# Differential attention: the query by key-low-part products as 64-row matmuls, both components scored in one step

## The chip, the cores and the metric

One core of one Trainium2 chip. The metric is the device time of one execution in microseconds (us), the median of several runs. TensorE (PE) multiplies, VectorE (DVE), ScalarE (ACT) and GpSimd (POOL) work on tiles of 128 partitions, and SyncE (SP) issues the transfers.

## What is computed

A block of two mixers over 2048 tokens of width 1024, followed by a sliding-window layer. The change lies in the first block's differential attention, with four heads of two components of 64 each:

```python
def diff_attention(q, k, v, lam, slopes):
    """q, k: (B,S,H,2,Dh) normalised; v: (B,S,H,2Dh). Returns (B,S,H,2Dh)."""
    ...
    def block(args):
        qblk, qp = args
        s = jnp.einsum('bqhce,bkhce->bchqk', qblk, k).astype(jnp.float32) * scale
        dist = jnp.abs(qp[:, None] - pos[None, :]).astype(jnp.float32)
        s = s - slopes[:, None, None] * dist
        a = jax.nn.softmax(s, axis=-1)
        w = a[:, 0] - lam * a[:, 1]
        return jnp.einsum('bhqk,bkhe->bqhe', w.astype(v.dtype), v)
```

So for each head and each block of 128 queries there are two score matrices of 128 x 2048, two softmaxes, their difference, and one product with v.

## The kernel before, in words

Every fp32 operand of a product is split into a high part and a low part, both in TensorE's rounded fp32, and a product is the sum of partial products in PSUM. Phase a projects x to q, k, v and z and writes the parts to DRAM. Phase b1 (`phase_b1`) is the differential attention, phase b2 (`phase_b2`) the dilated attention; then follow the output projection and the second layer.

Phase b1 goes through 64 steps g: 4 heads of 16 query tiles. The two components of a head are numbered e. A query tile `qst` holds component e's high part in partitions 0 to 63 and its low part in 64 to 127, for 512 queries. A key tile `kst` holds one part (i = 0 high, 1 low) of one component of 512 keys, twice: in partitions 0 to 63 and again in 64 to 127. One 128-row matmul therefore gives (q high + q low) times one key part, and two of them, accumulated, a score block of 128 x 512.

`scores(g, e, hf)` fills one PSUM tile `s_ps` of 128 x 1024, half hf of component e's row, with four matmuls (L322), and VectorE reads it once (L328): it adds the position bias, writes `et` in SBUF and keeps the running row maximum `mx`. There are four such fills in a step and 256 in the phase. The pool `b_ps` has two such tiles, so TensorE can fill one while VectorE reads the other. After both halves of a component, `exps` (L336, L338) applies the exponential on ScalarE; after both components, `combine` (L344 to L356) subtracts the weighted second from the first on GpSimd (in the last TAIL = 2 steps on VectorE).

Three steps later (LT = 3) `transposes` turns the result by 128 x 128 pieces on TensorE (L366), ScalarE writes the high part `pth` (L367) and VectorE the low part `ptl` (L368). Two steps after that `pv` (L380 to L382) multiplies with v, 24 matmuls of 256 columns a step. `evacuate` and `finish` (L386 to L414) normalise four tiles at a time: ScalarE, a chain of short VectorE instructions (`rsqrt_dve`, L238 to L256), GpSimd, and the store `s_y<-b_an`.

A list scheduler orders each engine's instructions when the program is built; the source's order is its priority. Loads go through SP's queue: `load_k` (L296) for a head, `load_q` (L309) for 512 queries, `load_v`.

Pools of a phase lie behind each other in SBUF in the order of its `with`. Phase b2's pools take the same addresses over, and one of them can be written only when the pools of b1 that lie there are free. The first three of b1, `b_c`, `b_q0` and `b_k0` (the bias, two query tiles, 20 key tiles), take 8.25 + 4 + 40 = 52.25 KB of a partition; behind them come `b_t2` (two `et` tiles of component 1), and later `b_v`, `b_p` (`pth`, `ptl`) and `b_o` (`b_ot`, `b_an`). Phase b2's first pool `d_h0` (queries, keys and values of a head) takes 41.5 KB and its second, `d_b` (the bias tables `d_nb`, `d_rb`, `d_two`), the next 9.25 KB; `d_p` (`d_nh`, `d_nl`, `d_ph`, `d_pl`) lies over `b_v` and `b_p`. Phase b2's `load` (L516 to L525) fetches a head, `scores_nat` (L541, L544) and `scores_res` (L564, L567) score it.

Of the kernel before, what the change touches and what calls it, by code (L numbers as in the profile page):

```python
# [16 lines left out]
P = 128  # L17
S = 2048
D = 1024
NT = S // P  # L20
# [2 lines left out]


def rsqrt_mean(nc, c, pool, ss, n, out=None):
    """1 / sqrt(ss / n + eps), refined by one Newton step."""
    w = ss.shape[-1]
    sd = pool.tile([P, w], F32, name="rm_sd")
    nc.scalar.activation(sd, ss, AF.Sqrt, bias=c["eps"], scale=1.0 / n)
    v = pool.tile([P, w], F32, name="rm_v")  # L30
    nc.vector.tensor_scalar(v, ss, 1.0 / n, EPS, ALU.mult, ALU.add)
    nc.vector.reciprocal(sd, sd)
    nc.vector.tensor_mul(v, v, sd)
    nc.vector.tensor_mul(v, v, sd)
# [196 lines left out]


def rsqrt_dve(nc, pool, ss, n, out=None):
    """1 / sqrt(ss / n + eps) on VectorE alone: exponent-halving start, three Newton steps (the
    first leaves -2 y, the second 16 y, and the third takes the factor out)."""
    w = ss.shape[-1]
    v = pool.tile([P, w], F32, name="rd_v")
    nc.vector.tensor_scalar(v, ss, 1.0 / n, EPS, ALU.mult, ALU.add)  # L238
    sh = pool.tile([P, w], I32, name="rd_i")
    nc.vector.tensor_scalar(sh, v.bitcast(I32), 1, None, ALU.logical_shift_right)  # L240
    y = pool.tile([P, w], F32, name="rd_y")
    nc.vector.tensor_scalar(y.bitcast(I32), sh, -1.0, float(0x5F3759DF), ALU.mult, ALU.add)
    a = pool.tile([P, w], F32, name="rd_a")
    if out is None:
        out = y
    for step in range(3):
        if w == 1:
            nc.vector.tensor_scalar(a, v, y, y, ALU.mult, ALU.mult)
        else:
            nc.vector.tensor_mul(a, y, y)  # L250
            nc.vector.tensor_mul(a, a, v)
        if step < 2:
            nc.vector.scalar_tensor_tensor(y, a, (3.0, 12.0)[step], y, ALU.subtract, ALU.mult)
        else:
            nc.vector.tensor_scalar(a, a, -0.5 / 4096, 1.5 / 16, ALU.mult, ALU.add)
            nc.vector.tensor_mul(out, y, a)  # L256
    return out


def phase_b1(tc, c, scr, ndist, sub_g, lam):  # L260
    nc = tc.nc
    NQ = 4 * NT
    with (
        tc.tile_pool(name="b_c", bufs=1) as cp,
        tc.tile_pool(name="b_q0", bufs=2) as qp0,
        tc.tile_pool(name="b_k0", bufs=20) as kp0,
        tc.tile_pool(name="b_t2", bufs=2) as tp2,
        tc.tile_pool(name="b_s", bufs=8) as sp,
        tc.tile_pool(name="b_t0", bufs=3) as tp0,
# [13 lines left out]
        bias = cp.tile([P, 3968], mybir.dt.float16, name="nd")  # L283
# [4 lines left out]

        heads, qts, st, pts, outs = {"n": 0}, {}, {}, {}, {}

        def load_k(h, e, j):
            for i in range(2):
                t = (kp0 if heads["n"] % 22 < 20 else kp1).tile([P, 512], F32R, name="kst")
                heads["n"] += 1
                for half in range(2):
                    nc.sync.dma_start(t[64 * half:64 * half + 64].bitcast(F32),  # L296
                                      scr["dk"][h, e, i][:, j * 512:j * 512 + 512])
                heads[h, "k", e, i, j] = t

        def load_v(h, j):  # L300
            t = vp.tile([P, 4, 2, 128], F32R, name="vt")
# [2 lines left out]
            heads[h, "v", j] = t  # L304

        def load_q(h, b):
            for e in range(2):
                t = (qp0, qp1)[b % 2].tile([P, 512], F32R, name="qst")
                nc.sync.dma_start(t.bitcast(F32),  # L309
                                  scr["dq"][h, e].rearrange("s d t -> (s d) t")[:, b * 512:b * 512 + 512])  # L310
                qts[h, b, e] = t

        def scores(g, e, hf):
            h, qt = divmod(g, NT)
            if e == 0 and hf == 0:
                st[g] = {"e": [pool.tile([P, 2, 1024], F32, name="et") for pool in (tp1 if g % 4 == 3 else tp0, tp3 if g % 3 == 2 else tp2)], "l": sp.tile([P, 2], F32, name="l")}
            et = st[g]["e"][e]
            lhs = qts[h, qt // 4, e][:, (qt % 4) * P:(qt % 4 + 1) * P]
            ps = ps_s.tile([P, 1024], F32, name="s_ps")
            for b in range(2):  # L320
                for i in range(2):
                    nc.tensor.matmul(ps[:, b * 512:b * 512 + 512], lhs, heads[h, "k", e, i, 2 * hf + b],  # L322
                                     start=i == 0, stop=i == 1)
            if hf == 0:
                st[g]["mx"] = sp.tile([P, 2], F32, name="mx")
            mx = st[g]["mx"]
            off = 1920 - qt * P + hf * 1024
            nc.vector.tensor_tensor_reduce(  # L328
                et[:, hf], ps, bias[:, off:off + 1024], 1.0,
                -3.0e38 if hf == 0 else mx[:, 0:1], ALU.add, ALU.max, mx[:, hf:hf + 1])  # L330

        def exps(g, e):
            slope = DIFF_SLOPES[g // NT]
            et, mx = st[g]["e"][e], st[g]["mx"]
            nm = sp.tile([P, 1], F32, name="nm")
            nc.scalar.activation(nm, mx[:, 1:2], AF.Copy, scale=-slope)  # L336
            ev = et.rearrange("p a k -> p (a k)")
            nc.scalar.activation(ev, ev, AF.Exp, bias=nm, scale=slope, accum_out=st[g]["l"][:, e:e + 1])  # L338
# [76 lines left out]
                    scr["y"][0][b * 512:(b + 1) * 512, h * 128:(h + 1) * 128].rearrange("(t p) w -> p t w", p=P), an)  # L415

        load_q(0, 0)
        for e in range(2):
            for j in range(4):
                load_k(0, e, j)  # L420
        for g in range(NQ + LT + 5):
            h, qt = divmod(g, NT)
            if g < NQ and qt == 0:
                for j in range(4):
                    load_v(h, j)
            if g < NQ and qt % 4 == 1:
                ng = g + 3
                if ng < NQ:
                    load_q(ng // NT, (ng % NT) // 4)
            for s in range(4):  # L430
                e, hf = divmod(s, 2)
                if g < NQ:
                    with tc.high_priority(offset=AHEAD) if g < EARLY else nullcontext():
                        scores(g, e, hf)
                    if qt == NT - 1 and h < 3 and hf == 1:
                        for j in range(4):
                            load_k(h + 1, e, j)
                if 0 <= g - LT < NQ:
                    transposes(g - LT, s)
                p, half = divmod(g - LT - 2, 2)  # L440
                if 0 <= p < NQ // 2:
                    for kt in range(8 * half + 2 * s, 8 * half + 2 * s + 2):
                        pv(p, kt)
                if s == FIN and half == 0 and 0 <= p - 1 < NQ // 2:
                    finish(p - 1)
                if g < NQ and hf == 1:
                    with tc.high_priority(offset=AHEAD) if g < EARLY else nullcontext():
                        exps(g, e)
            if g < NQ:
                with tc.high_priority(offset=AHEAD) if g < EARLY else nullcontext():  # L450
                    combine(g)
            p, half = divmod(g - LT - 2, 2)
            if half == 1 and 0 <= p < NQ // 2:
                evacuate(p)
# [312 lines left out]
def phase_c(tc, c, scr, x, p, w_out, ple_g, w_gate, w_proj, norm_g):  # L767
    nc = tc.nc
    with (
# [13 lines left out]
        wo, wg, wj = {}, {}, {}  # L783
# [6 lines left out]
            store[k, ch] = w  # L790

        def to_t(src_of, dst, cuts):
            """transpose 128-column pieces, cuts[i]:cuts[i + 1] at a time, and split them into dst[:, 0] and dst[:, 1]"""
            for b, m in zip(cuts, [e - b for b, e in zip(cuts, cuts[1:])]):
                ps = pt.tile([P, 4, P], F32, name="c_tp")
                for j in range(m):
                    nc.tensor.transpose(ps[:, j], src_of(b + j), c["id"])
                nc.scalar.activation(dst[:, 0, b:b + m], ps[:, :m], AF.Copy)
                nc.vector.tensor_sub(dst[:, 1, b:b + m], ps[:, :m], dst[:, 0, b:b + m].bitcast(F32))
# [529 lines left out]
```

## Time and profile before

| | us |
|---|---|
| median of 3 runs | 3122.9 (3122.07 to 3132.4) |
| profiled execution, span from first to last instruction | 3126.1 |
| PE busy (share of the span) | 2988.1 (96%) |
| weight loads busy | 2499.6 (80%) |
| DVE busy | 1980.9 (63%) |
| ACT busy | 1591.5 (51%) |
| POOL busy | 1165.9 (37%) |

The span is the profiled execution's own; nothing that lies around it is given apart. It is 3.2 us above the median of the runs and inside their spread. Busy time of PE is modelled with the matmuls' latency in it, so that a PE busy for 96% isn't at its peak. The shares are averages over stages: phase b1 lies from about 740 to 1450 us, phase b2 behind it to about 1850 us.

### The profile page before, as it was taken

What the parts mean: (1) busy time and instruction counts of PE and PEld (TensorE: products, weight loads), DVE (VectorE), ACT (ScalarE), POOL (GpSimd) and SP (SyncE); (2) the same over time, 40 slices, a digit from 0 to 9 for tenths busy, and PEclk for the clock granted to TensorE, in tenths of its full rate; (3) what the DMA queues carried; (4) which work ended last, traced back from release to release, by engine and by line L of the source; (5) the groups of instructions that cost most, each with busy time, mean ns of one, the idle gap of its engine ahead of it and who ended that gap; (6) DMA issues with size and microseconds to landing.
All of it is one profiled execution on the core that took longest, in us unless ns stands there. A gap on an engine that the chain in (4) does not pass through costs nothing.

```text
span 3126.1 us, 45716 instructions
## 1 busy us (share of the span) xinstructions
PE 2988.1 (96%) x15778; PEld 2499.6 (80%) x15778; DVE 1980.9 (63%) x4986; ACT 1591.5 (51%) x3528; POOL 1165.9 (37%) x1052
## 2 busy tenths in 40 slices
PE   8999999999988888988999989999999999999998
PEld 7788888887877777777887867888888888888787
DVE  4215555423999999997787765444445666666765
ACT  5223233312877666776877753222235666666621
POOL 1110011110876667763454540000035565555421
PEclk9999999999999999998999999999999999999999
DMA  7654444415131211106757563233273424232452
GB/s 211 126 132 102 104 118 118 111 61 174 30 91 39 81 55 48 54 15 154 173 143 163 123 167 112 88 107 105 89 238 97 155 88 155 88 116 80 130 190 84
DMA packets 421928, 352.78 MB, mean 113 GB/s; under 512 B 104480, under 2 KB 367168, under 8 KB 418624
## 3 DMA queue, kind: packets, MB, share of 16 engines
q1 hardware_dynamic: 421552, 348.83, 39.8%
q8 instruction: 126, 2.06, 0.3%
q0 software_dynamic: 144, 1.02, 0.2%
q14 instruction: 106, 0.87, 0.1%
HBM read 234.26 MB, written 116.52 MB: 112 GB/s over the span
## 4 chain that ended last, share of the span: by engine, by line
PE 80%; DVE 11%; DMA 4%; issue 2%; ACT 2%; SPq 1%; POOL 0%; DVEq 0%; ACTq 0%; POOLq 0%
PE psm L181 7%; PE psm L183 7%; PE psm L182 7%; PE e_mm L762 5%; PE e_mm L764 5%; PE s_ps L322 5%; PE e_mm L763 4%; PE c_mm L762 4%; PE c_mm L763 4%; PE c_mm L764 4%; DVE et L328 4%; PE d_sr L564 4%; PE t_ps L366 2%; PE f_mm L762 2%; PE f_mm L763 2%
## 5 line engine op out<-in xcount | busy, mean ns | idle before, releaser
L181 PE MATMUL psm<-w,hh 128*128 128x512 f32 x1024 | 406.3, 398 | 9.9 <-DVE t L111 7.1
L183 PE MATMUL psm<-w,hh 128*128 128x512 f32 x1024 | 399.5, 393 | 0.0
L182 PE MATMUL psm<-w,hl 128*128 128x512 f32 x1024 | 399.3, 391 | 0.0
L982 POOL TENSOR_TENSOR e_wt<-e_raw,e_wt 128x1024 fp32r<-128x1024 f32 x80 | 191.3, 2398 | 478.1 <-DMA e_raw<-in_a_w_in_dram 403.9
L322 PE MATMUL s_ps<-kst,qst 128*128 128x512 f32 x1024 | 309.3, 429 | 55.2 <-DVE mx L328 54.6
L101 POOL TENSOR_TENSOR w<-wraw,w 128x512 fp32r<-128x512 f32 x64 | 81.6, 1297 | 599.6 <-ACT w L100 589.6
L356 POOL TENSOR_TENSOR et<-et 128x1024 f32<-128x1024 f32 x124 | 295.1, 2401 | 0.0
L322 PEld LDWEIGHTS s_ps<-kst,qst 128*128 128x128 f32 x1024 | 187.3, 202 | 103.7 <-DVE mx L328 77.1
L338 ACT ACTIVATE et<-et,nm 128x2048 f32<-128x2048 f32 x128 | 257.0, 2007 | 5.7
L181 PEld LDWEIGHTS psm<-w,hh 128*128 128x128 f32 x1024 | 193.3, 189 | 48.5 <-DVE t L111 7.5
L762 PE MATMUL e_mm<-e_x,e_wt 128*128 128x512 f32 x576 | 228.1, 396 | 1.3 <-DVE e_k L1024 0.9
L764 PE MATMUL e_mm<-e_x,e_wt 128*128 128x512 f32 x576 | 226.8, 394 | 0.0
L763 PE MATMUL e_mm<-e_x,e_wt 128*128 128x512 f32 x576 | 226.6, 393 | 0.0
L183 PEld LDWEIGHTS psm<-w,hh 128*128 128x128 f32 x1024 | 192.9, 189 | 41.1
L182 PEld LDWEIGHTS psm<-w,hl 128*128 128x128 f32 x1024 | 193.7, 189 | 38.3
L355 POOL TENSOR_SCALAR et<-et,cc 128x1024 f32<-128x1024 f32 x124 | 138.4, 1131 | 215.8 <-DVE cc L346 122.9
L366 PE MATMUL t_ps<-id,et 128*128 128x128 f32 x1024 | 163.2, 289 | 21.0 <-DVE ptl L368 19.8
L1070 DVE CUSTOM_DVE_ANT_0 e_es<-e_s,e_bias,e_sk 128x256 f32<-128x256 f32 (+1 forms) x256 | 117.3, 472 | 104.1 <-PE e_s L1062 73.5
L1083 POOL TENSOR_SCALAR e_es<-e_es,e_l 128x256 f32<-128x256 f32 (+1 forms) x256 | 119.6, 488 | 170.2 <-DVE e_l L1081 105.2
L367 ACT ACTIVATE pth<-t_ps 128x512 fp32r<-128x512 f32 x256 | 146.4, 590 | 62.8 <-PE t_ps L366 57.7
L368 DVE TENSOR_TENSOR ptl<-t_ps,pth 128x512 fp32r<-128x512 f32 x256 | 170.5, 681 | 12.0 <-ACT pth L367 11.6
L328 DVE CUSTOM_DVE_ANT_0 et<-s_ps,nd,mx 128x1024 f32<-128x1024 f32 x128 | 163.5, 1277 | 19.9 <-PE s_ps L322 18.3
(265 smaller groups left out, 7936.6 us busy)
## 6 DMA issues: line engine op xcount, KB each, us to landing
e_raw<-in_a_w_in_dram SPq DMA_DIRECT2D x80, 512.0 KB, 3.6
wraw<-in_w_in_dram SPq DMA_DIRECT2D x64, 256.0 KB, 3.4
kst<-s_dk SPq DMA_DIRECT2D x128, 128.0 KB, 3.8
d_k<-s_bk SPq DMA_DIRECT2D x32, 512.0 KB, 12.0
s_xt<-c_at SPq DMA_DIRECT2D x32, 512.0 KB, 6.5
e_x<-s_xt SPq DMA_DIRECT2D x32, 512.0 KB, 6.9
t<-in_x_dram SPq DMA_DIRECT2D x32, 256.0 KB, 5.4
s_dv<-t SPq DMA_DIRECT2D x32, 256.0 KB, 3.1
```

The lines of the kernel that those rows point to most:

```text
L181: nc.tensor.matmul(ps, ah, cur[k][:, 0], start=k == 0, stop=False)
L182: nc.tensor.matmul(ps, al, cur[k][:, 0], start=False, stop=False)
L183: nc.tensor.matmul(ps, ah, cur[k][:, 1], start=False, stop=k == KD - 1)
L322: nc.tensor.matmul(ps[:, b * 512:b * 512 + 512], lhs, heads[h, "k", e, i, 2 * hf + b], start=i == 0, stop=i == 1)
L328: nc.vector.tensor_tensor_reduce(et[:, hf], ps, bias[:, off:off + 1024], 1.0, -3.0e38 if hf == 0 else mx[:, 0:1], ALU.add, ALU.max, mx[:, ...
L338: nc.scalar.activation(ev, ev, AF.Exp, bias=nm, scale=slope, accum_out=st[g]["l"][:, e:e + 1])
L356: nc.gpsimd.tensor_sub(es[0][:, hf], es[0][:, hf], es[1][:, hf])
L366: nc.tensor.transpose(pt[:, j], src[:, (4 * (kg % 2) + j) * P:(4 * (kg % 2) + j + 1) * P], c["id"])
L762: nc.tensor.matmul(ps, ah, bh, start=first, stop=False)
L763: nc.tensor.matmul(ps, al, bh, start=False, stop=False)
L764: nc.tensor.matmul(ps, ah, bl, start=False, stop=last)
L982: nc.gpsimd.tensor_sub(w[:, 1], raw, w[:, 0].bitcast(F32))
```

## The change

The low parts of the keys of both components go into one tile, component 0 in partitions 0 to 63 and component 1 in 64 to 127, and the low product uses the query's high part alone, with 64 rows: rows 0 to 63 for component 0, 64 to 127 for component 1. For this the query tile of component 1 is loaded with its parts exchanged. What is no longer computed is q low times k low. `scores` now fills two PSUM tiles, one of each component; a head has 12 key tiles for 16, and `b_k0` shrinks to 16 tiles.

```diff
-        tc.tile_pool(name="b_k0", bufs=20) as kp0,
+        tc.tile_pool(name="b_k0", bufs=16) as kp0,
...
-        def load_k(h, e, j):
-            for i in range(2):
-                t = (kp0 if heads["n"] % 22 < 20 else kp1).tile([P, 512], F32R, name="kst")
+        def load_k(h, j):
+
+            for nm, parts in (("k0", ((0, 0), (0, 0))), ("k1", ((1, 0), (1, 0))), ("kl", ((0, 1), (1, 1)))):
+                t = (kp0 if heads["n"] % 18 < 16 else kp1).tile([P, 512], F32R, name="kst")
                 heads["n"] += 1
-                for half in range(2):
+                for half, (e, i) in enumerate(parts):
                     nc.sync.dma_start(t[64 * half:64 * half + 64].bitcast(F32),
                                       scr["dk"][h, e, i][:, j * 512:j * 512 + 512])
-                heads[h, "k", e, i, j] = t
+                heads[h, nm, j] = t
...
             for e in range(2):
                 t = (qp0, qp1)[b % 2].tile([P, 512], F32R, name="qst")
-                nc.sync.dma_start(t.bitcast(F32),
-                                  scr["dq"][h, e].rearrange("s d t -> (s d) t")[:, b * 512:b * 512 + 512])
+                for i in range(2):
+                    half = i ^ e
+                    nc.sync.dma_start(t[64 * half:64 * half + 64].bitcast(F32),
+                                      scr["dq"][h, e, i][:, b * 512:b * 512 + 512])
                 qts[h, b, e] = t
...
-            ps = ps_s.tile([P, 1024], F32, name="s_ps")
+            lhs = [qts[h, qt // 4, e][:, (qt % 4) * P:(qt % 4 + 1) * P] for e in range(2)]
+            ps = [ps_s.tile([P, 1024], F32, name="s_ps") for _ in range(2)]
+            for e in range(2):
+                for b in range(2):
+                    nc.tensor.matmul(ps[e][:, b * 512:b * 512 + 512], lhs[e], heads[h, f"k{e}", 2 * hf + b],
+                                     start=True, stop=False)
             for b in range(2):
-                for i in range(2):
-                    nc.tensor.matmul(ps[:, b * 512:b * 512 + 512], lhs, heads[h, "k", e, i, 2 * hf + b],
-                                     start=i == 0, stop=i == 1)
...
+                for e in range(2):
+                    rows = slice(64 * e, 64 * e + 64)
+                    nc.tensor.matmul(ps[e][:, b * 512:b * 512 + 512], lhs[e][rows], heads[h, "kl", 2 * hf + b][rows],
+                                     start=False, stop=True)
             off = 1920 - qt * P + hf * 1024
-            nc.vector.tensor_tensor_reduce(
-                et[:, hf], ps, bias[:, off:off + 1024], 1.0,
-                -3.0e38 if hf == 0 else mx[:, 0:1], ALU.add, ALU.max, mx[:, hf:hf + 1])
+            for e in range(2):
+                mx = st[g]["mx"][e]
+                nc.vector.tensor_tensor_reduce(
+                    st[g]["e"][e][:, hf], ps[e], bias[:, off:off + 1024], 1.0,
+                    -3.0e38 if hf == 0 else mx[:, 0:1], ALU.add, ALU.max, mx[:, hf:hf + 1])
...
             for s in range(4):
-                e, hf = divmod(s, 2)
-                if g < NQ:
+                if g < NQ and s % 2 == 0:
                     with tc.high_priority(offset=AHEAD) if g < EARLY else nullcontext():
-                        scores(g, e, hf)
-                    if qt == NT - 1 and h < 3 and hf == 1:
-                        for j in range(4):
-                            load_k(h + 1, e, j)
+                        scores(g, s // 2)
+                    if qt == NT - 1 and h < 3:
+                        for j in range(s, s + 2):
+                            load_k(h + 1, j)
...
-                if g < NQ and hf == 1:
+                if g < NQ and s >= 2:
                     with tc.high_priority(offset=AHEAD) if g < EARLY else nullcontext():
-                        exps(g, e)
+                        exps(g, s - 2)
```

What the scheduler makes of it is read from the built programs. First, TensorE's queue in the middle of phase b1, before; `s_ps` is the PSUM tile that is filled, `kst` a key tile, `qst` a query tile, and the numbers tell tiles apart.

```order
L322 MATMUL s_ps_9810<-kst_8106,qst_9155 128x512
L322 MATMUL s_ps_9810<-kst_8109,qst_9155 128x512
L322 MATMUL s_ps_9810<-kst_8112,qst_9155 128x512
L322 MATMUL s_ps_9810<-kst_8115,qst_9155 128x512
L322 MATMUL s_ps_9845<-kst_8010,qst_9153 128x512
L322 MATMUL s_ps_9845<-kst_8013,qst_9153 128x512
L322 MATMUL s_ps_9845<-kst_8016,qst_9153 128x512
L322 MATMUL s_ps_9845<-kst_8019,qst_9153 128x512
L366 MATMUL t_ps_9854<-id_60,et_9508 128x128 x4
```

The same place now, two fills again; L327 are the 128-row products with the keys' high part, L332 the 64-row products.

```order
L375 MATMUL t_ps_8609<-id_60,et_8241 128x128 x4
L327 MATMUL s_ps_8597<-kst_7993,qst_8235 128x512
L327 MATMUL s_ps_8597<-kst_8002,qst_8235 128x512
L332 MATMUL s_ps_8597<-kst_7999,qst_8235 128x512
L332 MATMUL s_ps_8597<-kst_8008,qst_8235 128x512
L327 MATMUL s_ps_8598<-kst_7996,qst_8238 128x512
L327 MATMUL s_ps_8598<-kst_8005,qst_8238 128x512
L332 MATMUL s_ps_8598<-kst_7999,qst_8238 128x512
L332 MATMUL s_ps_8598<-kst_8008,qst_8238 128x512
L375 MATMUL t_ps_8622<-id_60,et_8241 128x128 x4
```

In the source the four 64-row products stand together, component 0 and 1 in turn. In the queue they stand tile by tile: two products of 128 rows, two of 64 rows in one half of the array, then the other component's. Over the whole phase the queue goes 514 times from 128 rows to 64 or back, and in 3 places a 64-row product of one component is next to one of the other.

Second, SP's queue where phase b1 ends, before (`d_q`, `d_k`, `d_vn`, `d_vr` are phase b2's first head, `d_nb` to `d_rb` its bias tables, `s_y` the stores of b1's output).

```order
L396 DMA b_sz<-s_sz 128x4x128
L487 DMA d_nb<-in_t_nat_dram 128x256
L489 DMA d_rb_14047<-in_t_res_dram 128x128
L491 DMA d_two<-in_t_two_dram 128x128
L495 DMA d_rb__14051<-in_t_res_dram 128x896
L495 DMA d_rb__14053<-in_t_res_dram 128x896
L516 DMA d_q<-s_bq 128x2048
L414 DMA s_y_137<-b_an 128x4x128
L519 DMA d_k_14057<-s_bk 64x2048 x2
```

And now:

```order
L526 DMA d_k_14042<-s_bk 64x2048 x2
L528 DMA d_vn_14045<-s_bv 128x15x128
L529 DMA d_vn_14045<-s_bv 64x128
L530 DMA d_vn_14045<-s_bv 64x128
L423 DMA s_y_137<-b_an 128x4x128
L532 DMA d_vr<-s_bv 128x16x128
L494 DMA d_nb<-in_t_nat_dram 128x256
L496 DMA d_rb_14031<-in_t_res_dram 128x128
```

The tables have moved behind the whole first head and behind a store, because `d_b` now lies over `b_t2`.

Third, ScalarE's queue at the first `d_ph` (phase b2's probabilities, pool `d_p`), with what the instructions wait for, before and now:

```order
L408 ACTIVATE b_j,b_ssq<-b_an 128x128 [waits Activation_49]
L599 ACTIVATE d_ph<-d_tr 128x4x128 [waits DMAHW1_49,PE_49]
L599 ACTIVATE d_ph<-d_tr 128x4x128 [waits PE_49]
L582 ACTIVATE d_pn<-d_tn 128x512 [waits PE_49,Pool_49]
L623 ACTIVATE d_o_14103<-d_ob 128x4x64 [waits PE_49]
```

```order
L422 ACTIVATE b_an<-b_an,rd_y 128x128 [waits DVE_49,Pool_49]
L422 ACTIVATE b_an<-b_an,rd_y 128x128 x2
L422 ACTIVATE b_an<-b_an,rd_y 128x128 [waits Activation_49]
L555 ACTIVATE d_en,d_o_14087<-d_en,d_nmn 128x256 [waits DVE_49,PE_49]
L555 ACTIVATE d_en,d_o_14087<-d_en,d_nmn 128x256
L606 ACTIVATE d_ph<-d_tr 128x4x128 [waits DMAHW3_49,DMAHW4_49,DMAHW1_49,DMAHW6_49,DMAHW0_49,Activation_49]
```

`d_p` now ends inside `b_o`, so that the first `d_ph` stands behind the last scaling of `b_an` (L422, L413 before) and waits for five queues of transfers, where it waited for one.

## Rows read from the trace of the kernel before

**Rows 1.** The page: each engine's busy time, share of the span, number of instructions.

```profile
PE 2988.1 (96%) x15778; PEld 2499.6 (80%) x15778; DVE 1980.9 (63%) x4986; ACT 1591.5 (51%) x3528; POOL 1165.9 (37%) x1052
```

**Rows 2.** Busy time by stretch: stretch and length, then busy us by engine, granted clock.

```profile
core 0: us, PE busy (x) PEld busy (x) DVE busy (x) ACT busy (x) POOL busy (x), PEclk, DMA share, GB/s
...
790.00:1420.00 630.00, 556.65 (x3416) 482.11 (x3417) 586.69 (x1019) 448.72 (x853) 455.71 (x270) 0.93 0.17 50
1420.00:1480.00 60.00, 49.46 (x296) 41.93 (x294) 42.30 (x146) 39.33 (x114) 13.90 (x14) 0.84 0.71 173
```

**Rows 3.** Groups by line, 790 to 1420 us: busy, mean ns; idle before, releaser.

```profile
L322 PE MATMUL s_ps<-kst,qst 128*128 128x512 f32 x959 | 289.4, 428 | 52.8 <-DVE mx L328 52.1
...
L328 DVE CUSTOM_DVE_ANT_0 et<-s_ps,nd,mx 128x1024 f32<-128x1024 f32 x120 | 153.3, 1277 | 19.2 <-PE s_ps L322 17.8
...
L328 DVE CUSTOM_DVE_ANT_0 et<-s_ps,nd 128x1024 f32<-128x1024 f32 x119 | 144.6, 1215 | 16.8 <-PE s_ps L322 13.6 <-POOL et L356 1.4 <-POOL et L355 0.6
```

**Rows 4.** Who waited for whom, 790 to 1420 us: total, times, longest.

```profile
PE s_ps L322 <- DVE mx L328: 52.1, 41, 5.0
...
DVE et L328 <- PE s_ps L322: 31.4, 50, 1.9
...
PE t_ps L366 <- DVE ptl L368: 17.1, 11, 2.7
...
DVE r L344 <- ACT et L338: 3.8, 10, 0.6
...
PE t_ps L405 <- DVE ptl L368: 3.7, 3, 1.2
```

**Rows 5.** The chain that ended last, 790 to 1420 us, shares by line.

```profile
by line: PE s_ps L322 21.8%; DVE et L328 18.0%; PE t_ps L366 9.7%; DVE ptl L368 7.4%; issue 7.2%; PE o_ps L380 5.4%; PE o_ps L381 5.3%; PE o_ps L382 5.3%; DVE rd_a L250 4.2%; DVE rd_a L251 3.4%; DVE rd_a L255 3.0%; DVE rd_y L242 2.5%; DVE r
```

**Rows 6.** Timeline of PE's matmuls in phase b2: start, us, line, rows*columns of the weights.

```profile
1823.06 0.28 PE L611 MATMUL d_or<-d_nl,d_vn 128*64 128x256 f32 x1
1823.17 0.28 PE L611 MATMUL d_or<-d_nh,d_vn 128*64 128x128 f32 x2
1823.29 0.22 PE L611 MATMUL d_or<-d_nl,d_vn 128*64 128x128 f32 x1
1823.45 0.46 PE L706 MATMUL d_ob<-id,d_ta 64*128 64x64 f32 x4
1823.83 2.10 PE L564 MATMUL d_sr<-d_k,d_q 128*128 128x512 f32 x4
```

**Rows 7.** The same view, another place in phase b2.

```profile
1504.81 0.22 PE L611 MATMUL d_or<-d_nl,d_vn 128*64 128x128 f32 x1
1504.87 1.16 PE L564 MATMUL d_sr<-d_k,d_q 128*128 128x512 f32 x2
1505.97 0.46 PE L706 MATMUL d_ob<-id,d_ta 64*128 64x64 f32 x4
1506.36 0.66 PE L579 MATMUL d_tn<-id,d_en 128*128 128x128 f32 x4
1506.85 0.60 PE L597 MATMUL d_tr<-id,d_er 128*128 128x128 f32 x4
```

**Rows 8.** Lines' instructions: ns min/median/max, first and last start; L322 in phase b1.

```profile
L322 PE MATMUL s_ps<-kst,qst x959: 387/393/797, 789.9 to 1419.6; 128*128 128x512 f32 x192
...
L706 PE MATMUL d_ob<-id,d_ta x128: 221/223/275, 1494.2 to 1842.3; 64*128 64x64 f32 x128
```

**Rows 9.** Timeline of all engines, a fill in phase b1.

```profile
1126.62 1.09 PE L322 MATMUL s_ps<-kst,qst 128*128 128x512 f32 x4
```

**Rows 10.** Timeline where phase b1 ends (brackets: idle before, releaser).

```profile
1423.74 1.27 DVE L328 CUSTOM_DVE_ANT_0 et<-s_ps,nd,mx 128x1024 f32<-128x1024 f32 x1
...
1440.76 0.55 PE L541 MATMUL d_sn<-d_k,d_q 128*128 128x256 f32 x1 [7.14 <-DMA d_k<-s_bk]
...
1446.98 0.42 DVE L544 CUSTOM_DVE_ANT_0 d_en<-d_sn,d_nb 128x256 f32<-128x256 f32 x1 [0.83 <-issue]
```

**Rows 11.** SP's queue in the same stretch: start, us in the queue.

```profile
1444.27 0.60 SPq L525 DMA_DIRECT2D d_vr<-s_bv  x1
1456.68 0.36 SPq L414 DMA_DIRECT2D s_y<-b_an  x1
...
1493.11 0.37 SPq L414 DMA_DIRECT2D s_y<-b_an  x1
```

**Rows 12.** The first d_ph on ACT: ns min/median/max, first and last start.

```profile
L599 ACT ACTIVATE d_ph<-d_tr x128: 574/597/607, 1468.0 to 1836.3; 128x512 fp32r<-128x512 f32 x128
```

**Rows 13.** Issues by line: count, KB each, median us to landing.

```profile
kst<-s_dk SPq DMA_DIRECT2D x128, 128.0 KB, 3.8
d_k<-s_bk SPq DMA_DIRECT2D x32, 512.0 KB, 12.0
...
s_y<-b_an SPq DMA_DIRECT2D x16, 256.0 KB, 2.3
```

More of the change, by code (lines that the diff above doesn't have):

```diff
@@ L308, in load_q, with scores @@
                 t = (qp0, qp1)[b % 2].tile([P, 512], F32R, name="qst")
-                nc.sync.dma_start(t.bitcast(F32),
-                                  scr["dq"][h, e].rearrange("s d t -> (s d) t")[:, b * 512:b * 512 + 512])
+                for i in range(2):
+                    half = i ^ e
+                    nc.sync.dma_start(t[64 * half:64 * half + 64].bitcast(F32),
+                                      scr["dq"][h, e, i][:, b * 512:b * 512 + 512])
                 qts[h, b, e] = t
-        def scores(g, e, hf):
+        def scores(g, hf):
@@ L314, in scores @@
             h, qt = divmod(g, NT)
[L315 to L318, printed above, removed]
-            ps = ps_s.tile([P, 1024], F32, name="s_ps")
-            for b in range(2):
-                for i in range(2):
-                    nc.tensor.matmul(ps[:, b * 512:b * 512 + 512], lhs, heads[h, "k", e, i, 2 * hf + b],
-                                     start=i == 0, stop=i == 1)
@@ L324, in scores @@
-            if hf == 0:
-                st[g]["mx"] = sp.tile([P, 2], F32, name="mx")
-            mx = st[g]["mx"]
-            off = 1920 - qt * P + hf * 1024
-            nc.vector.tensor_tensor_reduce(
-                et[:, hf], ps, bias[:, off:off + 1024], 1.0,
-                -3.0e38 if hf == 0 else mx[:, 0:1], ALU.add, ALU.max, mx[:, hf:hf + 1])
+            if hf == 0:
+                st[g] = {"e": [pool.tile([P, 2, 1024], F32, name="et") for pool in (tp1 if g % 4 == 3 else tp0, tp3 if g % 3 == 2 else tp2)],
+                         "l": sp.tile([P, 2], F32, name="l"),
+                         "mx": [sp.tile([P, 2], F32, name="mx") for _ in range(2)]}
@@ L332, in exps @@
+            off = 1920 - qt * P + hf * 1024
+            for e in range(2):
[3 more added lines that the diff above has]
+                    -3.0e38 if hf == 0 else mx[:, 0:1], ALU.add, ALU.max, mx[:, hf:hf + 1])
         def exps(g, e):
             slope = DIFF_SLOPES[g // NT]
-            et, mx = st[g]["e"][e], st[g]["mx"]
+            et, mx = st[g]["e"][e], st[g]["mx"][e]
@@ L417, in phase_b1 @@
         load_q(0, 0)
-        for e in range(2):
-            for j in range(4):
-                load_k(0, e, j)
+        for j in range(4):
+            load_k(0, j)
         for g in range(NQ + LT + 5):
@@ L430, in phase_b1 @@
             for s in range(4):
-                e, hf = divmod(s, 2)
-                if g < NQ:
+                if g < NQ and s % 2 == 0:
                     with tc.high_priority(offset=AHEAD) if g < EARLY else nullcontext():
-                        scores(g, e, hf)
-                    if qt == NT - 1 and h < 3 and hf == 1:
-                        for j in range(4):
-                            load_k(h + 1, e, j)
+                        scores(g, s // 2)
+                    if qt == NT - 1 and h < 3:
+                        for j in range(s, s + 2):
+                            load_k(h + 1, j)
                 if 0 <= g - LT < NQ:
```

## Prediction

> **What bounds the kernel now.** The page says that TensorE is busy for 96% of the span [rows 1], which is an average over stages, so the next view is the busy time of the stretch that the change lies in, 790 to 1420 us [rows 2]. There VectorE has 586.7 of 630 us and TensorE 556.7: neither is full, and the reader is to see two engines that hand the two PSUM tiles to and fro. The waits say how [rows 4]: TensorE waits 52.1 us for a reduction (`mx`) before a fill, in 41 waits, and 17.1 and 3.7 us for `ptl` before transposes, 72.9 us in all; VectorE waits 31.4 us for a fill. The chain through the stretch [rows 5] goes through both, 21.8% in the fills and 18.0% in the reductions. A microsecond taken from either is worth less than one here, and one added costs less than one.
>
> **What the change does to the matmuls.** The phase has 1024 score matmuls of 512 columns before and after; half of them now have 64 rows. A fill of four takes 1.09 us, its last one 0.39 [rows 8, 9], so one step is (1.09 - 0.39) / 3 = 0.23 us. The trace has no 64-row matmul of 512 columns. Steps in it go with the columns: 0.06 us for 128, 0.11 for 256 [rows 6]. So I take 0.23 for 64 rows too, and a gain of 0 from the rows alone. The other end is that the two halves of the array work side by side: then 256 pairs save 256 x 0.23 = 59 us of TensorE. That needs the two components' low products next to each other in the queue, and the built queue has them so in 3 places; everywhere else the scheduler has finished one PSUM tile before it begins the other, because the second tile comes free only when VectorE has read it.
>
> **What it adds: 514 changes between 128 and 64 rows.** Before, phase b1 has none. Phase b2 has some, in the 64-row transposes of `d_ob`. The last 128-column matmul ahead of one starts at 1823.29 and the transpose at 1823.45 [rows 6]: 0.16 us, where its neighbours of the same size take 0.06. That is 0.10 us of nothing. On the way back, the fourth transpose starts 0.46 - 0.22 = 0.24 us after the first [rows 6, 8], at 1823.69, and the next 128-row matmul at 1823.83, 0.14 later for 64 columns, which should take at most 0.06: 0.08 or more. Rows 7 repeat this (1506.21 to 1506.36). I take 0.09 a change. Behind a change the first weight load isn't hidden: four transposes take 0.66 us and the next four 0.60 [rows 7], which is 0.06 more. A change costs 0.09 + 0.06 = 0.15 us, and 514 of them 77.1 us of TensorE. A change of columns costs nothing (64 to 128 columns from 1504.81 to 1504.87, the plain step of 0.06 [rows 7]), so it is the rows.
>
> The Trainium skill, TensorEngine Tiling (Array Packing), Key Properties, says that changing the tiling mode, and not just the tile, drains TensorE. For rows the trace agrees, with the 0.09 us; for columns it doesn't, with the 0.06 us that is a plain step. By that rule the gap belongs to each of the 514 changes and not to a wait of the transposes, which is the more reason to take it for all.
>
> **How much of it lies on the path.** The chain has 21.8% of 630 us, 137.3 us, in the fills [rows 5], of 289.4 us that they are busy [rows 3]: 47%. In that share of the fills TensorE is the one that is late, and what is added there moves the end; in the rest it waits for VectorE anyway. 0.47 x 77.1 = 36 us. The ends are 77.1 - 72.9 = 4 us, if all of TensorE's idle time took up what is added, and 77 us, if nothing did. I take 36, by the row that is about these very instructions. The granted clock is 0.93 in the stretch [rows 2], so some of it runs at 1.2 GHz instead of 2.4 and a change may cost more there than in phase b2; the upper end has room for it.
>
> **The reductions and exponentials.** Their number and sizes stay (1277 and 1215 ns [rows 3]). Component 0's exponential now follows the third reduction of a step instead of the second, and component 1's comes right behind it. The result is read three steps later, and a step takes 630 / 60 = 10.5 us (239 reductions at 4 a step), so I cost this at 0; if that cover were too short, VectorE's wait for ScalarE (3.8 us [rows 4]) would double: +4.
>
> **The loads.** `kst` goes from 128 to 96 issues, `qst` from 32 of 256 KB to 64 of 128 KB. The transfer engines are at 0.17 in the stretch [rows 2] and no wait for a key tile stands in rows 4: cost 0, at worst one landing of 3.8 us [rows 13] at each of 3 changes of head, 11 us.
>
> **Where the phase ends.** Four key tiles fewer move all later pools by 8 KB. Two things follow in the built order. First, phase b2's tables are loaded behind its first head and a store. The first head can't come earlier, since its queries wait for the last reduction, at 1423.74 [rows 10], as before, and TensorE's wait of 7.14 us for `d_k` stays. Its last load is issued at 1444.27 [rows 11]; tables behind it land about when they are first used, 1446.98 [rows 10]. Second, the first `d_ph`, at 1468.0 [rows 12], 44.3 us after the last reduction, now waits for the last stores of b1's output. The last but one store is issued 32.9 us after that reduction (1456.68 [rows 11]). The last may follow after the TensorE work of four more tiles without scores, 64 transposes of at most 0.60 / 4 = 0.15 us [rows 7] and 96 products of 256 columns at 0.11 [rows 6]: 20.2 us, so 53.1 us after the reduction. It lands 2.3 us later if the queue is free and 12.0 us later if it stands behind a head's keys [rows 13]: 55.4 to 65.1, which is 11 to 21 us behind the old 44.3. Behind `d_ph` on ScalarE stand exponentials and the copies `d_pn`, for which GpSimd and then TensorE's products with v wait; the scores of b2 need none of them and cover some of it. I take 12, nearer to the free queue, since the store is small; ends 0 and 21.
>
> **Sum.** 36 + 0 + 0 + 12 = 48 us. Against the profiled execution 3126.1 + 48 = 3174; that one lies 3.2 us above the median of the runs, so in their terms **3122.9 + 48 = 3171 us**.
>
> **Rivals.**
> - *TensorE's idle time takes the changes up.* Then only 4 + 12 = 16 us are left: 3139. For it: 72.9 us of idle against 77.1 added. Against it: the idle comes in 41 long waits [rows 4] for some 240 fills, and what is added comes in every fill. With the end of the phase free as well it is 4 us: 3127, no change that can be told.
> - *TensorE becomes the bound.* Some 240 of the 256 fills lie in the stretch [rows 3], so 556.7 + 240 / 256 x 77.1 = 629 of 630 us. If VectorE's stalls still add to that, nothing is hidden: 77 + 21 = 98 us, 3221. Against it: VectorE's waits and TensorE's partly fall together.
> - *The halves do work side by side, and it is faster.* Place: the low products; price: 59 us less for TensorE, of which VectorE, at 93%, passes on at most its waits for a fill, 31.4 us [rows 4]. With 12 us lost at the end: 3122.9 - 31.4 + 12 = 3104. It decides from the point where most of the 256 pairs stand next to each other, or where the hardware overlaps a 64-row product with a 128-row one of the other tile; the first is so in 3 places, and for the second no row speaks: [rows 6, 7] show 64 and 128 rows strictly behind each other.
>
> On the third, the Trainium skill, TensorE: Matmul & The Clock Gate, Part 3, says that matmuls in different row groups of the array run at the same time, some 4 ns apart. No run here shows it, and by it the sum would be that rival's 3104, had the queue kept the pairs.
>
> **Chances.** The forecast 0.60, taken up 0.18 with the phase's end and 0.05 without it, TensorE the bound 0.11, side by side 0.06. About 0.3% (9 us) is what a measurement of this kernel can tell from no change. Slower by more: 0.60 + 0.18 + 0.11 = 0.89; the same 0.05; faster 0.06. The range begins below the first rival's 3139, at 3137, and ends at 3212, where all 77 us and the 12 us count: it leaves out no change, faster, and the upper part of the bound case, some 0.2.
>
> **What would show it.** PSUM fills of two components never overlap; each fill's four matmuls take about 1.09 + 0.15 us, and the next matmul starts 0.15 us late; TensorE's waits for `mx` fall from 52 us well below 30, VectorE's for fills rise above 31; the stretch from the first to the last reduction is some 36 us longer; the first `d_ph` comes about 56 us after the last reduction. Steps of 0.11 us among the 64-row products would make the forecast wrong, as would a change of rows without a gap, or TensorE's waits as long as before.

## The result and the profile after

The changed kernel takes **3236.9 us** (median of 4 runs, 3233.5 to 3248.7), 1.036 times before (95% interval 1.0334 to 1.0386): 112 us slower between the profiled executions. The forecast was 3171, its range went from 3137 to 3212. One run of the kernel before (6304 us) and one of e8 (3314 us) were slow executions and stand in no ratio; beside the experiments the kernel before took 3126.9 to 3128.5 us, and the table has it with 3127.

First the busy time of the stretch from the first to the last reduction, the same work in both: the line of before, in a stretch that [rows 2] does not have, then that of after.

```profile
core 0: us, PE busy (x) PEld busy (x) DVE busy (x) ACT busy (x) POOL busy (x), PEclk, DMA share, GB/s
744.70:1423.80 679.10, 599.35 (x3594) 514.22 (x3592) 618.54 (x1077) 472.28 (x886) 467.76 (x278) 0.93 0.20 58
```

```profile
745.30:1514.20 768.90, 719.91 (x3586) 496.87 (x3584) 608.28 (x1068) 468.14 (x877) 466.08 (x278) 0.88 0.14 44
```

The stretch grew by 89.8 us. TensorE is busy 120.6 us longer in it and idle 49.0 us instead of 79.7. VectorE has nearly the same work. And the granted clock fell from 0.93 to 0.88. Each fill is what the forecast priced; the view is PE's timeline, as in [rows 9].

```profile
1160.13 0.63 PE L327 MATMUL s_ps<-kst,qst 128*128 128x512 f32 x2
1160.68 0.73 PE L332 MATMUL s_ps<-kst,qst 64*128 64x512 f32 x2
1161.34 0.66 PE L375 MATMUL t_ps<-id,et 128*128 128x128 f32 x4
```

From the first score matmul to the transposes behind the fill it is 1.21 us; four plain steps of 0.23 are 0.92, so two changes of rows cost 0.29. Two waits over the whole stretch, before and then after (the stretch of [rows 4] is shorter):

```profile
PE s_ps L322 <- DVE mx L328: 54.6, 45, 5.0
...
DVE et L328 <- PE s_ps L322: 32.0, 51, 1.9
```

```profile
DVE et L337 <- PE s_ps L332: 103.0, 93, 2.8
...
PE s_ps L327 <- DVE mx L337: 43.9, 32, 4.5
```

VectorE waits three times as long for fills (103.0 us for 32.0), while TensorE's wait for reductions fell only from 54.6 to 43.9. The end of the phase, against [rows 10 to 12]: the last reduction, the last store on SP's queue and the first `d_ph`, from three views of after.

```profile
1514.24 1.27 DVE L337 CUSTOM_DVE_ANT_0 et<-s_ps,nd,mx 128x1024 f32<-128x1024 f32 x1
```

```profile
1562.55 2.30 SPq L423 DMA_DIRECT2D s_y<-b_an  x1
```

```profile
L606 ACT ACTIVATE d_ph<-d_tr x128: 570/595/624, 1569.3 to 1946.9; 128x512 fp32r<-128x512 f32 x128
```

The first `d_ph` stands 55.1 us behind the last reduction (44.2 before), 6.8 behind the issue of the last store. From the first to the last `d_ph` it is 377.6 us, before 368.3 [rows 12]. So the 112 us are 0.6 ahead of the stretch, 89.8 in it, 10.9 to the first `d_ph`, 9.3 to the last and 1.4 behind.

**The clock.** The trace's record of the clock has 16 falls from 2.4 to 1.2 GHz in the stretch before and 14 after, mostly one every 35 to 55 us, about as often as a finish of four query tiles ends. They are not more, but longer: 5.8 us on average before, 13.4 after. One of each kernel, ahead of it, in it and behind it:

```profile
1070.00:1074.80 4.80, 1.66 (x11) 1.11 (x10) 4.77 (x12) 1.01 (x5) 4.03 (x4) 0.99 0.50 169
1074.80:1081.60 6.80, 5.82 (x16) 3.92 (x15) 6.80 (x9) 5.00 (x14) 3.87 (x2) 0.50 0.29 95
1081.60:1086.00 4.40, 4.40 (x32) 3.89 (x31) 4.11 (x10) 3.67 (x7) 0.00 (x0) 1.00 0.92 216
```

```profile
1120.00:1125.10 5.10, 2.65 (x8) 1.07 (x9) 5.07 (x7) 3.74 (x8) 4.35 (x2) 1.00 0.34 97
1125.10:1142.20 17.10, 16.62 (x51) 11.03 (x52) 10.37 (x22) 10.52 (x21) 6.90 (x4) 0.50 0.28 86
1142.20:1147.00 4.80, 4.80 (x28) 3.33 (x27) 2.50 (x6) 0.80 (x2) 4.25 (x3) 1.00 0.00 0
```

Ahead of these two TensorE was busy 1.66 of 4.8 and 2.65 of 5.1 us. The first lasts 6.8 us, the second 17.1. What VectorE did in the pause of the kernel before, and GpSimd at the same time:

```profile
1068.74 2.30 DVE L250 TENSOR_TENSOR rd_a<-rd_y 128x4 f32<-128x4 f32 x1
```

```profile
1068.64 2.39 POOL L356 TENSOR_TENSOR et<-et 128x1024 f32<-128x1024 f32 x1
```

An operation on four elements of each partition takes 2.30 us (the shortest of its line 0.14) and ends when GpSimd's ends, 1071.04 and 1071.03. It belongs to the inverse square root in `finish`, a chain of 13 such operations. Behind it stand the `ptl` copies and reductions that TensorE waits for. Every fall of both kernels but the first follows a pause of TensorE with operations of this chain just ahead of it.

**How the stretch adds up.** At a mean clock c a busy TensorE loses (1 - c) of the stretch. This is an estimate that takes TensorE as busy in the falls: 47.5 us before, 92.3 after (clocks have two digits, so either is good to 4 us; half the length of the falls gives 46.5 and 93.9). Busy time less that loss is its work at full clock: 551.8 and 627.6. So: 75.8 us more work, 44.8 more lost to the clock, 30.7 of idle time taken up; 75.8 + 44.8 - 30.7 = 89.9. The same sum for all kernels, from the line of that view for each (us):

| kernel | median | stretch | PE busy | clock | work | idle |
|---|---|---|---|---|---|---|
| before | 3127 | 679.1 | 599.4 | 0.93 | 552 | 80 |
| changed | 3236.9 | 768.9 | 719.9 | 0.88 | 628 | 49 |
| e1 new order, 128 rows | 3117.6 | 671.4 | 600.4 | 0.93 | 553 | 71 |
| e2 old order, 64 rows | 3203.2 | 753.5 | 710.0 | 0.89 | 627 | 44 |
| e3 same, 4 changes a fill | 3264.8 | 808.3 | 797.0 | 0.91 | 724 | 11 |
| e4 changed, 20 key tiles | 3225.7 | 782.7 | 735.8 | 0.86 | 626 | 47 |
| e5 changed, no root | 3117.2 | 644.3 | 639.5 | 0.99 | 633 | 5 |
| e6 before, no root | 3056.5 | 611.2 | 570.9 | 0.97 | 553 | 40 |
| e7 one PSUM tile, pairs | 3202.4 | 742.9 | 616.5 | 0.90 | 542 | 126 |
| e8 one PSUM tile, 128 rows | 3208.7 | 760.4 | 632.6 | 0.92 | 572 | 128 |
| e9 e1, root on GpSimd | 3019.6 | 572.0 | 558.3 | 1.00 | 558 | 14 |
| e10 before, root on GpSimd | 3023.5 | 570.5 | 558.3 | 0.99 | 553 | 12 |
| e11 changed, root on GpSimd | 3117.4 | 645.4 | 640.7 | 0.99 | 634 | 5 |
| e12 e11, 20 key tiles | 3114.9 | 652.7 | 645.6 | 0.98 | 633 | 7 |

The sum has its limits: e8 has the same matmuls as e1 and comes out with 18 us more work. The mean fall tells with and without row changes apart: 5.8 us before and 6.6 in e1, but 11.7 in e2, 10.8 in e3, 13.4 in the changed kernel and 14.8 in e4. It does not grow with their number, since e3 has twice as many as e2.

### The profile page after: what moved, and what is told of

Read it like the earlier page. It is cut to its first block, busy times and chain, and to the rows that moved or that the text cites. A ratio compares the mean times of both kernels' runs of the same rounds, so it can differ in the third digit from the quotient of the medians.

```text
span 3238.1 us, 45668 instructions
## 1 busy us (share of the span) xinstructions
PE 3120.0 (96%) x15778; PEld 2489.2 (77%) x15778; DVE 1972.8 (61%) x4986; ACT 1591.1 (49%) x3528; POOL 1163.0 (36%) x1052
## 4 chain that ended last, share of the span: by engine, by line
PE 81%; DVE 10%; DMA 4%; ACT 2%; SPq 2%; issue 1%; POOL 0%; DVEq 0%; ACTq 0%; POOLq 0%
PE psm L181 7%; PE psm L183 7%; PE psm L182 7%; PE e_mm L769 4%; PE e_mm L771 4%; PE e_mm L770 4%; PE s_ps L332 4%; PE c_mm L769 4%; PE c_mm L771 4%; PE c_mm L770 4%; PE s_ps L327 3%; PE d_sr L571 3%; DVE et L337 3%; PE t_ps L375 3%; PE f_mm L770 2%; PE f_mm L771 2%
## 5 line engine op out<-in xcount | busy, mean ns | idle before, releaser
L327 PE MATMUL s_ps<-kst,qst 128*128 128x512 f32 x512 | 196.1, 468 | 43.9 <-DVE mx L337 43.9
L181 PEld LDWEIGHTS psm<-w,hh 128*128 128x128 f32 x1024 | 193.4, 189 | 47.2 <-DVE t L111 7.7
L332 PE MATMUL s_ps<-kst,qst 64*128 64x512 f32 x512 | 209.7, 493 | 0.0
L337 DVE CUSTOM_DVE_ANT_0 et<-s_ps,nd 128x1024 f32<-128x1024 f32 x128 | 155.2, 1220 | 71.5 <-PE s_ps L332 42.1
```

Of the source, the lines that this page charges most:

```text
L181: nc.tensor.matmul(ps, ah, cur[k][:, 0], start=k == 0, stop=False)
L327: nc.tensor.matmul(ps[e][:, b * 512:b * 512 + 512], lhs[e], heads[h, f"k{e}", 2 * hf + b], start=True, stop=False)
L332: nc.tensor.matmul(ps[e][:, b * 512:b * 512 + 512], lhs[e][rows], heads[h, "kl", 2 * hf + b][rows], start=False, stop=True)
L337: nc.vector.tensor_tensor_reduce(st[g]["e"][e][:, hf], ps[e], bias[:, off:off + 1024], 1.0, -3.0e38 if hf == 0 else mx[:, 0:1], ALU.add, A ...
```

## The experiments

**e1: the new order alone.** From the changed kernel, with 20 key tiles:

```diff
-for nm, parts in (..., ("kl", ((0, 1), (1, 1)))):
+for nm, parts in (..., ("l0", ((0, 1), (0, 1))), ("l1", ((1, 1), (1, 1)))):
...
-rows = slice(64 * e, 64 * e + 64)
-nc.tensor.matmul(..., lhs[e][rows], heads[h, "kl", 2 * hf + b][rows],
+nc.tensor.matmul(..., lhs[e], heads[h, f"l{e}", 2 * hf + b],
```

> The changed kernel with its order (both components scored together, component 0's exponential later), but with all 128 rows in the low products too, each from a tile of its own, and 20 key tiles as before. Theory A (the changes between 128 and 64 rows make the loss in the stage): the time falls back to that of before, 3120 to 3135 us; the granted clock from the first to the last reduction is 0.93 again, TensorE's busy time there 600 us. Rival B (the new order makes it: two tiles wanted at once, a later exponential): most of the 90 us of the stage stays, 3180 us or more, with VectorE's waits for fills near the 103 us of the changed kernel.

3117.6 us, 0.9972 of before (0.9961 to 0.9983), work 553 us, clock 0.93. The order is not the loss; it is a small gain.

**e2 and e3: the row changes alone, two and four a fill.** From the kernel before; e2 has the loops over `i` and `b` exchanged, e3 has not:

```diff
-    nc.tensor.matmul(..., lhs, heads[h, "k", e, i, 2 * hf + b],
+    rows = slice(0, 128 - 64 * i)
+    nc.tensor.matmul(..., lhs[rows], heads[h, "k", e, i, 2 * hf + b][rows],
```

> The kernel before, one component at a time, with nothing changed but that the two low products of a fill stand last and use 64 rows: two changes of rows in each of 256 fills, and no pair in different halves. Theory A: nearly the whole loss of the stage, 70 to 95 us, 3195 to 3220; TensorE busier by about 120 us between the first and the last reduction (77 by the changes, the rest by the clock). Rival B (the order): 0 to 20 us. My prediction's share (47% of 77 us on the path, the rest in the wait for reductions): 36 us, 3160.

> As the one with 64-row low products alone, but high and low products alternate: four changes of rows in a fill instead of two. Theory A: the alternating matmuls at 738.79 to 742.44 us of the changed kernel stand 0.43 us apart where 0.23 is a plain step, 0.20 for each change; 1024 of them make 205 us, of which TensorE's idle time can take 50 to 80: 125 to 155 us over before, and more with a lower clock, 3245 to 3310. Rival C (a 64-row matmul of 512 columns is itself slower, and the change costs nothing): the same time as with two changes.

3203.2 us (1.0244, 1.0228 to 1.0259) and 3264.8 (1.0436, 1.0416 to 1.0456): as theory A has it. The trace of e2 has 514 changes, that of e3 1020. The work grew by 75 us, 0.147 for each change (0.147 for the changed kernel's 514 too), and by 172, 0.169 for each. The stretch of e2:

```profile
745.10:1498.60 753.50, 709.95 (x3596) 490.29 (x3595) 605.95 (x1077) 478.85 (x888) 466.69 (x278) 0.89 0.17 52
```

Rival C falls: with the same 64-row matmuls, twice the changes make the difference. e3 leaves TensorE 11 us of idle time: 172 us more work and 25 more lost to the clock, less 69 of idle time taken up, make the 129 us by which its stretch is longer than before.

**e4: the pools where they were.** From the changed kernel:

```diff
-tc.tile_pool(name="b_k0", bufs=16) as kp0,
+tc.tile_pool(name="b_k0", bufs=20) as kp0,
...
-t = (kp0 if heads["n"] % 18 < 16 else kp1)
+t = (kp0 if heads["n"] % 22 < 20 else kp1)
```

> The changed kernel with 20 and 2 key tiles instead of 16 and 2, so that the later pools lie where they lay before. The loss at the phase's end (first d_ph 55.1 us after the last reduction, 44.3 before) should go: first d_ph about 44 us after it, and 10 to 20 us less in all, 3217 to 3227. If the end of the phase is late for another reason (the fills, the clock), it stays within 0.3% of the changed kernel.

3225.7 us, 11 less, as expected. The first `d_ph` comes 48.2 us behind the last reduction (about 44 were expected) and the last one 411.5 (changed kernel 432.7, before 412.5), so the end of the phase gives back 21 us. The stretch takes 13.8 us more, at a clock of 0.86: the rest is lost there.

**e5 and e6: the chain of small operations left out.** In the changed kernel and in the kernel before; the root and its Newton steps are not computed:

```diff
-rs = rsqrt_dve(nc, fp, ssq, 128)
+rs = fp.tile([P, 4], F32, name="rs")
+nc.vector.tensor_scalar(rs, ssq, 1.0 / 128, EPS, ALU.mult, ALU.add)
```

> The changed kernel without the inverse square root of the sub-norm: the thirteen short VectorE operations in each finish of four query tiles become one (mean square plus eps is used as the factor, the root and the Newton steps are left out). The clock falls come about every 42 to 50 us, as often as a finish, each behind a pause of TensorE while VectorE sits in that chain. Theory D (the pauses set the falls off, the row changes only make each last longer): the granted clock from first to last reduction rises from 0.88 to 0.95 or more and the time falls by 45 to 80 us, to 3155 to 3190. Rival E (the 64-row work itself pulls the clock down): it stays below 0.90, and only VectorE's chain is saved, some 20 to 30 us, 3205 to 3220.

> The kernel before with the same part left out (root and Newton steps of the sub-norm). It is the base for the changed kernel without that chain. By theory D the clock goes from 0.93 to 0.97 or more, and the difference between the two falls from 112 us to what the 77 us of changes are worth without clock falls: 77 less 31 to 50 us of TensorE's idle time, and 11 to 20 at the phase's end: 40 to 65 us. By E the difference stays near 110 us. Its own time: 3085 to 3115.

3117.2 and 3056.5 us. The stretches of e5 and e6:

```profile
747.80:1392.10 644.30, 639.47 (x3567) 447.24 (x3566) 492.22 (x903) 464.60 (x880) 467.08 (x278) 0.99 0.18 53
```

```profile
748.10:1359.30 611.20, 570.85 (x3602) 496.94 (x3601) 525.61 (x911) 471.00 (x892) 467.65 (x278) 0.97 0.23 65
```

The changed kernel's clock goes to 0.99 with one fall left, so theory D stands and E falls: row changes without the pauses don't pull the clock down. The difference is 61 us by the medians, as expected, and 51 between the profiled executions, 33 of them in the stretch. Both gain far more than expected, 120 and 71. In e6 seven falls remain, and the one operation that is left still takes 2.76 us on average, for four elements of each partition:

```profile
L411 DVE TENSOR_SCALAR rs<-b_ssq 128x4 f32<-128x4 f32 x14 | 38.6, 2760 | 0.0
```

**e7 and e8: pairs that stand together.** From the changed kernel (e7) and from e1 (e8, no row changes):

```diff
-tc.tile_pool(name="b_ps", bufs=2, space=PSUM) as ps_s,
+tc.tile_pool(name="b_ps", bufs=1, space=PSUM) as ps_s,
...
-ps = [ps_s.tile([P, 1024], F32, name="s_ps") for _ in range(2)]
+ps = ps_s.tile([P, 2, 1024], F32, name="s_ps")
...
```

> The changed kernel with both components in one PSUM tile of four banks (one buffer) instead of two tiles of two banks. The four 64-row low products of a half step then stand together in the queue, one of each component in turn, 128 fills with two row changes each instead of 256. If the two halves of the array work side by side when neighbours lie in different halves: steps of about 0.00 and 0.23 us in turn among the four, TensorE needs 128 x (6 x 0.23 + 0.30) = 215 us for the scores where before takes 235 and the changed kernel 313. If they don't: 128 x (8 x 0.23 + 0.30) = 274 us. Reductions and fills can no longer overlap: 1.7 + 2.5 us a half step in series, of 5.3 that there are now, so the time is open: 3060 to 3180 with pairs, 40 us more without.

> The same with one PSUM tile of four banks, but all low products with 128 rows (from tiles of their own, 20 key tiles): no row change, no pair. TensorE needs 128 x 8 x 0.23 = 235 us for the scores. With pairs side by side it should be 10 to 20 us slower than the kernel with pairs in one tile; with no such pairs, 20 to 38 us faster.

PE's timeline in e7, then in e8:

```profile
1008.42 1.10 PE L327 MATMUL s_ps<-kst,qst 128*128 128x512 f32 x4
1009.46 0.73 PE L332 MATMUL s_ps<-kst,qst 64*128 64x512 f32 x4
1010.12 0.39 PE L391 MATMUL o_ps<-ptl,vt 128*128 128x256 f32 x1
```

```profile
1018.69 1.09 PE L328 MATMUL s_ps<-kst,qst 128*128 128x512 f32 x4
1019.62 1.08 PE L332 MATMUL s_ps<-kst,qst 128*128 128x512 f32 x4
1020.54 0.28 PE L391 MATMUL o_ps<-ptl,vt 128*128 128x256 f32 x1
```

Four 64-row products of alternating halves take 0.66 us, as long as two in the changed kernel (1160.68 to 1161.34); at 128 rows they take 0.92. The halves do work side by side once they are neighbours. Both changes included, eight products take 1.70 us against 1.85. TensorE's work is 30 us less than in e8 (20 was reckoned). It buys 6 us, where 10 to 20 were expected. The two differ in the pools as well: e8 has 20 key tiles, and of the 17.5 us by which e7's stretch is shorter, 9 are lost up to the last `d_ph`. With one PSUM tile TensorE is idle for 126 us, 75 of them in waits for reductions, and both kernels are slower than before (1.0232, 1.0212 to 1.0251; 1.0248, 1.0225 to 1.027). The time of e7 missed what was expected, 3060 to 3180. Each has 26 falls of the clock in the stretch, many with no operation of the chain just ahead: a pause of another origin does as well.

**e9 to e11: the root on GpSimd.** Every result is computed; from e1, the kernel before and the changed kernel. VectorE keeps the two integer operations:

```diff
+def rsqrt_pool(nc, pool, ss, n):
+    w = ss.shape[-1]
+    v = pool.tile([P, w], F32, name="rd_v")
+    nc.gpsimd.tensor_scalar(v, ss, 1.0 / n, EPS, ALU.mult, ALU.add)
+    sh = pool.tile([P, w], I32, name="rd_i")
+    nc.vector.tensor_scalar(sh, v.bitcast(I32), 1, None, ALU.logical_shift_right)
+    y = pool.tile([P, w], F32, name="rd_y")
+    nc.vector.tensor_scalar(y.bitcast(I32), sh, -1.0, float(0x5F3759DF), ALU.mult, ALU.add)
+    a = pool.tile([P, w], F32, name="rd_a")
+    for _ in range(3):
+        nc.gpsimd.tensor_mul(a, y, y)
+        nc.gpsimd.tensor_mul(a, a, v)
+        nc.gpsimd.tensor_scalar(a, a, -0.5, 1.5, ALU.mult, ALU.add)
+        nc.gpsimd.tensor_mul(y, y, a)
+    return y
...
-rs = rsqrt_dve(nc, fp, ssq, 128)
+rs = rsqrt_pool(nc, fp, ssq, 128)
```

> A candidate to beat both: both components scored together with 128-row low products (0.997 of before by itself), and the inverse square root of the sub-norm computed whole, but with its Newton steps on GpSimd and only the two integer operations on VectorE. If the pauses behind VectorE's chain are what pulls the clock down, most of the 71 us that leaving the chain out saved comes back: 3050 to 3085 us, clock 0.96 or more in the stage. If the chain on GpSimd delays the combinations in its queue instead: 3110 to 3130.

> The kernel before with the same inverse square root on GpSimd. It tells the two parts of the candidate apart: 0 to 12 us slower than the candidate if the order with both components is worth the same here as alone, and 3055 to 3090 us.

> The changed kernel with the same inverse square root on GpSimd: the comparison without the chain on VectorE once more, with every result computed. Theory D: 50 to 65 us slower than the kernel before with the same chain (61 where it was left out), and TensorE's busy time within 10 us of the whole stretch between first and last reduction, at a clock of 0.97 or more. Theory E: 100 us or more.

**e9 beats both kernels: 3019.6 us**, 0.9656 of before (0.9637 to 0.9674). e10 takes 3023.5 (0.9666, 0.965 to 0.9682), so the new order is worth too little here to be told apart. Both are some 30 us below the least that was expected (3050 and 3055). e11 takes 3117.4, 94 more than e10; 50 to 65 were expected, and that was wrong. The lines of the stretch, e10 and e11:

```profile
744.70:1315.20 570.50, 558.28 (x3593) 487.35 (x3592) 497.09 (x921) 464.99 (x886) 500.19 (x451) 0.99 0.24 68
```

```profile
748.80:1394.20 645.40, 640.71 (x3582) 448.33 (x3581) 512.23 (x919) 465.29 (x878) 499.80 (x458) 0.99 0.18 53
```

Both run at 0.99, so only some 6 us are lost to the clock, but TensorE had only 12 us of idle time left in e10, and 75 of 82 us of changes lengthen the stretch. The other 19 us are the end of the phase and b2.

**e12: e11 with the pools where they were** (the edit of e4).

> The changed kernel with the inverse square root on GpSimd (3117.4 us) and 20 key tiles, so that the later pools lie as before. With the clock out of the way (0.99 in the stage) the pools' share shows by itself: from the last reduction to the last d_ph 412 to 416 us as in the kernels with 20 key tiles, where the changed kernel takes 433 to 435, so about 20 us less, 3094 to 3102. If the lower clock alone had lengthened the end of the phase, the time stays at 3117.

3114.9 us, 2.5 less and too little to be told apart, not 20. The first `d_ph` comes at 48.5 us (54.3 in e11, 47.2 in e10) and the last at 425.6 (434.7, 415.2): 9 us came back, and the stretch took 7 more, as e4's took 14 more. So the pools explain 6 to 7 us of the first `d_ph`'s delay, in e4 as here, and some of what follows. They are not its only cause: in e3, with the pools of before, it comes at 50.4 us. Why the stretch is longer with 20 key tiles, and what holds b2's remaining 10 us, stays open.

## Why the prediction was wrong

- **64-row products as long as 128-row ones, no pairing: right.** The pairs were not neighbours, and where they are (e7) the rival's mechanism is real. The Trainium skill, TensorE: Matmul & The Clock Gate, Part 3, says so of matmuls in different row groups; by e7's rows (four in the time of two) the trace agrees.
- **A change costs 0.15 us, 77.1 in all: right.** By the estimate above 75.8, good to some 8, or 0.147 each, in e2 as well. The Trainium skill, TensorEngine Tiling (Array Packing), Key Properties, has the drain at a change of mode; e2 and e3 agree for rows, with 0.15 and 0.17 us each.
- **47% of it on the path, 36 us: the step that failed.** It said: "The granted clock is 0.93 in the stretch, so some of it runs at 1.2 GHz instead of 2.4 and a change may cost more there than in phase b2; the upper end has room for it." The clock was taken as given. With the changes the falls are longer, and that cost TensorE another 45 us, on all its work in the falls and not on the changes alone. Of the 121 us together 31 were taken up by idle time and 90 reached the end. With the clock as it was, 75.8 - 30.7 would be 45 us, near my 36. From e6 to e5 the stretch grew by 33, and 12 us that e6 loses more to its clock stand against it: 45 again without them. But that it is near 36 is luck, since the share is no constant: from e10 to e11 75 of 82 us reach the end, for want of idle time.
- **The upper end, 77 us: wrong for the same reason.** The bound case, 3221, came nearest, and even it had no clock in it.
- **Reductions and exponentials 0: nearly right.** e1 is 9 us faster.
- **Loads 0: right** for their number; no key tile is waited for beyond 0.9 us.
- **End of the phase 12 us: right in place and size up to the first `d_ph`**, 55.1 us behind the last reduction where 56 was forecast. But by e4 the pools make only 6.9 of these 10.9 us, so that the size fits is in part luck. The 9 us that b2 lost besides were not in the sum.
- **What would have shown it:** the fill (1.21 for 1.24 us), VectorE's waits and the first `d_ph` came as forecast. TensorE's wait for `mx`, 43.9 instead of well below 30, spoke against the share, and so did the stretch, longer by 89.8 us instead of 36.

Shown by e5, e9, e10 and e11: with the chain away from VectorE, one fall is left in the stretch, with row changes or without (three in e12). That it is by the pauses and not by another effect of the chain is read from the traces; e7 and e8 speak for it. Not shown: why a fall lasts longer with row changes, and why longest in e4, which has the same matmuls as the changed kernel.

## What to carry to other kernels

Where the granted clock is below 1 in a stage, its falls are a term of the sum: what is added to TensorE can lengthen them, and then all matmuls in the falls pay. How much of an added cost reaches the end follows from the idle time that is left and not from a share of the chain. And half-height matmuls can pay only if they stand in pairs and at least two pairs share a change of rows and the way back: a pair saves 0.23 us here, the two changes cost 0.29.

## What was not expected

VectorE's operations on four elements of each partition were one of its largest costs. Three of the eight groups in the stretch, before:

```profile
L250 DVE TENSOR_TENSOR rd_a<-rd_y 128x4 f32<-128x4 f32 x42 | 30.3, 720 | 0.2
L251 DVE TENSOR_TENSOR rd_a<-rd_a,rd_v 128x4 f32<-128x4 f32 x42 | 23.9, 568 | 0.5
L255 DVE TENSOR_SCALAR rd_a<-rd_a 128x4 f32<-128x4 f32 x14 | 20.2, 1442 | 0.1
```

All eight make 148 us in 14 finishes, where the shortest operations of these three lines take 0.14 us; at 0.15 each the 182 would take 27. They count as busy time, so [rows 2] showed VectorE at 93% with a fifth of it, some 120 us, spent standing beside GpSimd's long operations. The Trainium skill, GPSIMD Engine Reference, Specifications, says that GpSimd's interfaces to SBUF are shared with VectorE and that VectorE instructions with two SBUF inputs are among those that contend; the rows at 1068.74 and 1068.64 us agree, with 2.30 us for a product of two operands in SBUF. Moving the chain gave 105 us (e10), nearly what the change under study cost, 109 by the medians.
